# Strassen block products for twelve of 22 row tiles of a feed-forward down-projection, and for two more groups of the up-projection

## The chip, the cores and the metric

The kernel runs on one core of a Trainium2 chip. The metric is device microseconds of that core for one execution. TensorE multiplies matrices and writes to PSUM, which has eight banks of 128 x 512 fp32 here; VectorE (DVE), ScalarE (ACT) and GpSimd (POOL) work on tiles of 128 partitions; SyncE (SP) issues all DMAs.

## The reference

One layer of a model of width 1024 over 1024 tokens: RMS norm, a large input projection, sparse attention (8 heads) and an RWKV-7 recurrence side by side, their gated sum, an output projection with residual, and last a feed-forward part. Only the last is changed:

```python
def _conv_ffn(h, w_up, conv_w, w_down):
    u = h @ w_up                      # [1024, 1024] x [1024, 5632]
    u = causal depthwise convolution of u over tokens, width 3
    a, b = jnp.split(u, 2, axis=-1)   # 2816 columns each
    return (jax.nn.silu(a) * b) @ w_down   # [2816, 1024]

x = x + _conv_ffn(_rms_norm(x, norm_ffn), ffn_up, ffn_conv, ffn_down)
```

All is fp32.

## The kernel before, in words

**Precision.** Each fp32 operand is split in two fp32r tiles: hi is a ScalarE copy to fp32r, lo is the difference x - hi, on GpSimd for weights (lines 219, 1328) and on VectorE or GpSimd for data. A product is three matmuls of 128 x 128 by 128 x 512: hi hi, hi lo and lo hi (`mm3`, line 222). Tokens lie on the free axis in two halves of 512, h = 0 and 1.

**Order.** Instructions get a place on their engine from a planner, by priority (`tc.cur_priority`, program order within it) and the times it assumes; `tc.issue_after(x)` holds an instruction back behind x. Each engine then runs its list in order. A tile that takes the memory of another waits for that one's last reader.

**Up-projection.** The 2816 + 2816 columns are 22 groups: group i has output column tiles i and 22 + i (o = 0, 1), over k = 8 row tiles. The first `NE` = 12 groups are plain. Their half 0 is done by `ffn0(i)` (line 709), early: groups 0 to 7 (`NEW` = 8) as filler behind the recurrence, groups 8 to 11 at line 1250, at a lower priority than the norm of half 1 (lines 1238 to 1245), so that TensorE has work while VectorE, ScalarE and GpSimd normalize. Their half 1 is the loop at line 1341, one group after the other. Weights come as 512 KB tiles, three ahead, through `wslot` into a ring of four hi/lo slots, of which two lie in the pool `wp`, two in the pool `ffn` (opened at line 1255, when the norm's pools are closed). Raw weights alternate between two buffers in each pool (`wraw`). `taps` evacuates a bank with the convolution (one ScalarE and two VectorE operations of 512 columns, and two small ones for half 1), `silu` makes the gate and stores it to `th_d` in DRAM.

**Strassen groups.** Groups 12 to 21 are done for both halves at once by a Winograd form of Strassen's scheme: the weights as a 2 x 2 block matrix (output o by half of k), the data as one (half of k by token half), 7 block products in place of 8, 12 matmuls each (`prod`, loop at line 1394). Sums of weight blocks (`s12`, `s34`) are made by `prep_up`, sums of data blocks T1 to T4 once by `tprep` (per k tile 12 VectorE operations of 512 columns: 4 `summed`, 4 `diff`, 4 low parts), spread over the half-1 loop by `tsteps`.

**Down-projection** (line 1434). 22 row tiles in pairs. For each pair two gate tiles per half are loaded (`thr`), cut into hi (ScalarE, line 1445) and lo (GpSimd, line 1446), two weight tiles go through `wslot`, and 8 x 2 outputs of 6 matmuls each go through the banks of P and B (four); VectorE adds each bank to one of 16 running sums `acc` (line 1464), which begin as the residual `x2`. The last pair stores them.

Of the kernel before, what the change touches and what calls it, by code (L numbers as in the profile page):

```python
# [38 lines left out]
NZS = 3  # L39
# [92 lines left out]
def build(tc, D, dbg=None, upto=99):  # L132
# [7 lines left out]
    with ExitStack() as ctx:  # L140
# [1115 lines left out]

        def taps(u, o, i, h, pj, prev):
            ci = 22 * o + i
            A.activation(u, pj, AF.Copy, scale=P("conv", 88 + ci))  # L1259
            for d in (1, 2):  # L1260
                cw_ = P("conv", 44 * (2 - d) + ci)
                V.scalar_tensor_tensor(u[:, d:512], pj[:, 0:512 - d], cw_, u[:, d:512], op0=ALU.mult, op1=ALU.add)  # L1262
                if h:
                    V.scalar_tensor_tensor(u[:, 0:d], prev(d), cw_, u[:, 0:d], op0=ALU.mult, op1=ALU.add)  # L1264

        def silu(i, h, ua, ub):
            th = fp.tile([128, 512], F32, name="th", bufs=2)
# [72 lines left out]
        wq = [wslot(D["f_up"][22 * (n % 2) + n // 2]) for n in range(PFD)]  # L1340
        for i in range(NE):
            us = []
            for o in range(2):
                n = 2 * i + o + PFD
                if n < 2 * NE:
                    wq.append(wslot(D["f_up"][22 * (n % 2) + n // 2]))
                hi, lo = wq.pop(0)
                u = utile(o, 1)
                pj = ps("AM"[o])
                mm3(pj, hi, lo, h2hi[1], h2lo[1], 8)  # L1350
                taps(u, o, i, 1, pj, lambda d: cvl[:, i, o, 2 - d:2])
                us.append(u)
            t_ = silu(i, 1, *us)
            with tc.issue_after(t_):
                for k in tsteps[i]:
                    next(tg[k])

        def prod(bank, w, o_, xs_, start):
            n = 0
            for k, wi, xi in [(k, 0, x_) for k in range(4) for x_ in (0, 1)] + [(k, 1, 0) for k in range(4)]:  # L1360
                T.matmul(bank, w[wi][:, o_ + k], xs_[k][xi], start=start and n == 0, stop=n == 11,  # L1361
                         skip_group_check=True)
                n += 1

        b11 = [(h2hi[0][k], h2lo[0][k]) for k in range(4)]
        b21 = [(h2hi[0][k], h2lo[0][k]) for k in range(4, 8)]
        b22 = [(h2hi[1][k], h2lo[1][k]) for k in range(4, 8)]
        lo4, hi4 = slice(0, 4), slice(4, 8)

        def prep_up(i):  # L1370
# [13 lines left out]
            w["b"] = split8(rb, wp, wp, "whi", "wlo", hi4, bufs=2)  # L1384
            yield

        def tmp(name, tag, n):
            return FP["f"].tile([128, 512], F32, name=name, tag=tag, bufs=n)

        g_ = prep_up(NE)  # L1390
        w = next(g_)
        for _ in range(3):
            next(g_)
        for i in range(NE, 22):
            g_ = prep_up(i + 1) if i < 21 else iter([None] * 4)
            pa, pb, pc, pd_ = ps("P"), ps("M"), ps("A"), ps("B")
            prod(pa, w["a"], 0, b11, True)
            p1 = tmp("p1", "zs", NZS)
            A.activation(p1, pa, AF.Copy)
            prod(pb, w["12"], 4, TB[2], True)  # L1400
            u2 = tmp("u2", "fu", 3)
            V.tensor_add(u2, pb, p1)  # L1402
            prod(pa, w["a"], 4, b21, False)
            wn = next(g_)
# [12 lines left out]
            prod(pb, w["b"], 4, TB[4], False)  # L1417
            next(g_)
            V.tensor_add(pb, pb, p1)
            taps(u[1][0], 1, i, 0, pb, None)  # L1420
# [5 lines left out]
        acc = {}  # L1426
        for m in range(8):
            for h in range(2):
                if m < 4:
                    acc[m, h] = hp2.tile([128, 512], F32, name=f"acc{m}{h}", tag=f"{('h2hi', 'h2lo')[h]}_{m}")  # L1430
                else:
                    acc[m, h] = fp.tile([128, 512], F32, name=f"acc{m}{h}", tag=f"T3{'hl'[h]}{m - 4}")
        GR = 2
        for g0 in range(0, 22, GR):
            hd_, wd_ = [], []
            for i in range(g0, g0 + GR):
                raw = fp.tile([128, 2, 512], F32, name="thr", tag=("s12", "s34")[i % 2])
                j = i % 4
                hs = []
                for h in range(2):  # L1440
                    load(raw[:, h], th_d[h][i])
                    tn = (2, 1)[j // 2], 2 * (j % 2) + h
                    hi = fp.tile([128, 512], FR, name="hh", tag="T%dh%d" % tn)
                    lo = fp.tile([128, 512], FR, name="hl", tag="T%dl%d" % tn)
                    A.activation(hi, raw[:, h], AF.Copy)  # L1445
                    G.tensor_sub(lo, raw[:, h], hi.bitcast(F32))  # L1446
                    hs.append((hi, lo))
                hd_.append(hs)
                wd_.append(wslot(D["f_dn"][i]))
            if g0 == 0:  # L1450
                with tc.issue_after(lastw[0]):
                    for m in range(8):
                        for h in range(2):
                            load(acc[m, h], x2_d[h][m])
            for m in range(8):
                for h in range(2):
                    pj = ps("PB"[h])
                    n = 0
                    for hs, (dh, dl) in zip(hd_, wd_):
                        hh, hl = hs[h]  # L1460
                        for a, b in ((dh, hh), (dh, hl), (dl, hh)):
                            T.matmul(pj, a[:, m], b, start=(n == 0), stop=(n == 3 * GR - 1))  # L1462
                            n += 1
                    V.tensor_add(acc[m, h], acc[m, h], pj)  # L1464
                    if g0 + GR >= 22:
                        nc.sync.dma_start(D["out"][m][:, H[h]], acc[m, h])
        fst.close()
        hst[1].close()

# [16 lines left out]
```

## Time and profile before

| | before |
|---|---|
| runs, median (lowest to highest) | 1855.0 us (1852.8 to 1855.7), 3 runs |
| the profiled execution | 1852.6 us, of which 1850.8 us is the span of the profile |
| mean granted TensorE clock | 0.989 of 2.4 GHz |
| TensorE busy | 1786.8 us, 97% of the span |
| VectorE, ScalarE, GpSimd busy | 1100.7, 824.4, 706.2 us |

The span goes from the first to the last instruction. Busy time of matmuls counts pipelined instructions, so a busy TensorE still needs the count beside it: matmuls started per microsecond. A wait is shown with what ended it. In the rows, L225 is line 225 of the kernel; names such as `psP` are tiles (`psP`: a PSUM bank with tag P), the form follows as output from input.

### The profile page before, as it was taken

The numbers are of one execution on the slowest core, as the hardware profiler recorded it, in microseconds if no ns is written. First come the engines' busy times: TensorE is split into PE (matmuls) and PEld (weight loads), VectorE is DVE, ScalarE is ACT, GpSimd is POOL, SyncE is SP. The second block draws the span as 40 slices with busy tenths as digits, with TensorE's granted clock in tenths as the row PEclk, the third lists the DMA queues.
The fourth block names the chain that finished last, engine by engine and source line by source line (L and its number), as shares of the span: only waits on it lengthen the run. The fifth ranks groups of instructions, "written<-read, shape, count | busy, mean of one in ns | idle before, by whom it ended". The sixth has DMA issues, their size and how long they took to land. (4 is left out here: it accounts for less than half of the span.)

```text
span 1850.8 us, 30936 instructions
## 1 busy us (share of the span) xinstructions
PE 1786.8 (97%) x11986; PEld 1389.8 (75%) x11986; DVE 1100.7 (59%) x1933; ACT 824.4 (45%) x1512; POOL 706.2 (38%) x454
## 2 busy tenths in 40 slices
PE   8999999999999999999999899999999999999999
PEld 5885657777777787777777678878877888888887
DVE  6214666768766503974444354347998988844444
ACT  5234765657555632545555454343344444411220
POOL 5222032141233335212145455555443444644441
PEclk9999999999999999999999899999999999999999
DMA  5415053232333346255453465334332223622222
GB/s 177 125 52 186 29 170 96 81 114 60 125 132 126 126 136 229 97 172 169 158 171 120 144 226 167 123 108 143 114 114 91 80 80 102 240 91 92 91 69 91
DMA packets 134019, 232.29 MB, mean 126 GB/s; under 512 B 25072, under 2 KB 54128, under 8 KB 133616
## 3 DMA queue, kind: packets, MB, share of 16 engines
q1 hardware_dynamic: 133872, 230.31, 38.0%
q8 instruction: 94, 1.54, 0.3%
q14 instruction: 53, 0.43, 0.1%
HBM read 161.48 MB, written 63.96 MB: 122 GB/s over the span
## 5 line engine op out<-in xcount | busy, mean ns | idle before, releaser
L219 POOL TENSOR_TENSOR wlo<-wraw,whi 128x1024 fp32r<-128x1024 f32 (+1 forms) x110 | 241.2, 2197 | 419.8 <-ACT whi L218 147.5
L225 PE MATMUL psP<-hhi,whi 128*128 128x512 f32 x816 | 333.6, 410 | 14.0 <-ACT hhi L705 8.1
L225 PE MATMUL psP<-hlo,whi 128*128 128x512 f32 x816 | 330.1, 405 | 3.8 <-DVE hlo L706 2.5
L225 PE MATMUL psP<-hhi,wlo 128*128 128x512 f32 x816 | 215.2, 397 | 0.0
L225 PEld LDWEIGHTS psP<-hhi,whi 128*128 128x128 f32 x816 | 156.2, 192 | 52.6 <-ACT hhi L705 9.9
L225 PEld LDWEIGHTS psP<-hlo,whi 128*128 128x128 f32 x816 | 156.5, 192 | 40.3 <-DVE hlo L706 3.8
L225 PEld LDWEIGHTS psP<-hhi,wlo 128*128 128x128 f32 x816 | 151.1, 188 | 32.7 <-issue 0.5
L218 ACT ACTIVATE whi<-wraw 128x1024 fp32r<-128x1024 f32 (+1 forms) x110 | 106.0, 964 | 130.0 <-PE psP L225 79.9
L542 DVE TENSOR_TENSOR pl<-pf,ph 128x512 f16<-128x512 f32 (+3 forms) x208 | 123.6, 603 | 43.8 <-ACT pf L541 42.9
L540 ACT ACTIVATE ph<-psA 128x512 f16<-128x512 f32 (+3 forms) x208 | 99.2, 477 | 61.7 <-PE psA L535 43.4
L483 DVE TENSOR_REDUCE mp<-psM 128x1 f32<-128x512 f32 (+1 forms) x192 | 94.4, 514 | 42.7 <-PE psM L481 35.9
L1328 POOL TENSOR_TENSOR wlo<-wraw,whi 128x1024 fp32r<-128x1024 f32 (+1 forms) x43 | 99.0, 2302 | 44.9 <-ACT whi L1327 32.6
L1446 POOL TENSOR_TENSOR hl<-thr,hh 128x512 fp32r<-128x512 f32 x44 | 57.9, 1329 | 114.8 <-ACT hh L1445 114.8
L1445 ACT ACTIVATE hh<-thr 128x512 fp32r<-128x512 f32 x44 | 27.2, 625 | 163.9 <-PE psB L1462 160.3
L541 ACT ACTIVATE pf<-psA 128x512 f32<-128x512 f32 (+3 forms) x208 | 99.7, 479 | 0.0
L1464 DVE TENSOR_TENSOR acc<-acc,psP 128x512 f32<-128x512 f32 x88 | 60.5, 687 | 59.3 <-PE psP L1462 59.3
L1464 DVE TENSOR_TENSOR acc<-acc,psB 128x512 f32<-128x512 f32 x88 | 60.5, 687 | 59.3 <-PE psB L1462 59.3
L545 PEld LDWEIGHTS <-ph 128*128 128x128 f16 x592 | 55.8, 97 | 22.5 <-issue 12.5
L550 PEld LDWEIGHTS <-pl 128*128 128x128 f16 x592 | 55.4, 98 | 20.5 <-DVE pl L542 6.3
L564 POOL TENSOR_TENSOR onat<-onat,ot 128x256 f32<-128x256 f32 x32 | 25.0, 783 | 111.8 <-DVE ot L563 88.8
L720 DVE SCALAR_TENSOR_TENSOR fu<-psP,par,fu 128x511 f32<-128x511 f32 (+1 forms) x48 | 35.8, 747 | 41.1 <-ACT cvl L718 40.4
L1269 ACT ACTIVATE th<-u 128x512 f32<-128x512 f32 x32 | 20.1, 627 | 84.8 <-issue 70.5
(472 smaller groups left out, 4594.4 us busy)
## 6 DMA issues: line engine op xcount, KB each, us to landing
wraw<-f_up SPq DMA_DIRECT2D x68, 512.0 KB, 3.4
wraw<-w_t SPq DMA_DIRECT2D x46, 512.0 KB, 3.9
wraw<-f_dn SPq DMA_DIRECT2D x22, 512.0 KB, 4.1
thr<-th_d SPq DMA_DIRECT2D x44, 256.0 KB, 4.1
sg_d<-zs SPq DMA_DIRECT2D x32, 256.0 KB, 2.0
wraw<-w_out SPq DMA_DIRECT2D x16, 512.0 KB, 3.4
th_d<-th SPq DMA_DIRECT2D x32, 256.0 KB, 2.1
z_d<-zs SPq DMA_DIRECT2D x28, 256.0 KB, 2.4
```

Of the source, the lines that this page charges most:

```text
L218: A.activation(hi[:, :nk], raw, AF.Copy)
L219: G.tensor_sub(lo[:, :nk], raw, hi[:, :nk].bitcast(F32))
L225: T.matmul(ps, a[:, k], ks_(b, k), start=(n == 0), stop=(n == 3 * nk - 1))
L483: V.reduce_max(mp[:, x, br, t:t + 1], pm[:, 0:(b1 - b0) * 128], axis=AX.X)
L540: A.activation(ph[0:nkey, rg], pa[0:nkey, rg], AF.Exp, scale=0.125)
L541: A.activation(pf[0:nkey, rg], pa[0:nkey, rg], AF.Exp, scale=0.125)
L542: V.tensor_sub(pl[0:nkey, rg], pf[0:nkey, rg], ph[0:nkey, rg])
L545: T.matmul(pov[:, t, :], ph[0:nkey, tk], vt[0:nkey, kb, g, 0:65], start=first, stop=False, skip_group_check=True)
L550: T.matmul(pov[:, t, :], pl[0:nkey, tk], vt[0:nkey, kb, g, 0:65], start=False, stop=True, skip_group_check=True)
L1328: G.tensor_sub(lo[:, ks], raw[:, ks], hi[:, ks].bitcast(F32))
L1446: G.tensor_sub(lo, raw[:, h], hi.bitcast(F32))
L1464: V.tensor_add(acc[m, h], acc[m, h], pj)
```

## The change

`NE` goes from 12 to 10: groups 10 and 11 of the up-projection become Strassen groups; `ffn0` and the half-1 loop have two groups less. The twelve entries of `tsteps` become ten. In the half-1 loop the gate of group i - 1 comes behind the taps of group i, and the first Strassen group's weights are prepared in the loop's last round.

The down-projection goes through `DSEQ` = "nnsnsnsn": n is a plain pair of row tiles (`plain`), s is a set of four (`combined`), so 5 x 2 plain and 3 x 4 combined. In a set the weights are a 2 x 2 block matrix (row tiles by output half), the gates another (row tiles by token half). There are 7 products of 4 outputs with 6 matmuls each: `product(o1)` ("a"), o2, o5 ("e"), o6 ("b"), o7 ("d"), o3, o4. o2, o3 and o4 are added to `acc` at once; the four others have running sums `sacc` over the three sets (the first set copies them by ScalarE), which `merge` adds into `acc` in the last set. `operands` cuts weights (ScalarE, GpSimd) and data (ScalarE, and GpSimd or VectorE); block sums are made on VectorE, queued in `todo` and let go one by one behind the bank sums (`tick`). All eight banks are used in turn, for plain pairs too. Rings: four weight slots, twelve places for data.

```diff
-NE, NEW = 12, 8
+NE, NEW = 10, 8
+DSEQ = "nnsnsnsn"
...
-        tsteps = [(), (0,), (0,), (0, 1), (1,), (), (1, 2), (2,), (2, 3), (3,), (3,), ()]
+        tsteps = [(), (0,), (0,), (0, 1), (1,), (1, 2), (2,), (2, 3), (3,), (3,)]
...
         for i in range(NE):
             us = []
+            if i == NE - 1:
+                g_ = prep_up(NE)
+                w = next(g_)
+                next(g_)
             for o in range(2):
...
-            t_ = silu(i, 1, *us)
-            with tc.issue_after(t_):
+            if i:
+                silu(i - 1, 1, *prev)
+            prev = us
+            with tc.issue_after(lasts[0]):
                 for k in tsteps[i]:
                     next(tg[k])
+        silu(NE - 1, 1, *prev)
...
+        def tick(ins):
+            if todo:
+                with tc.issue_after(ins.ins):
+                    todo.pop(0)()
...
+        def cut(dst, src, e):
+            A.activation(dst[0], src, AF.Copy)
+            e.tensor_sub(dst[1], src, dst[0].bitcast(F32))
...
+        def combined(i0, first, last):
...
+            def sums(n_):
+                for kp in range(2):
+                    def tsum(kp=kp):
+                        b11, b12, b21, b22 = B[kp]
+                        t = tt[kp][n_] = f32t(FP["f"], FT, [128, 512], "tq")
+                        x, y = ((b12, b11), (b22, tt[kp][0]), (b22, b12), (b21, tt[kp][1]))[n_]
+                        V.tensor_sub(t, x, y)
...
+                    todo.extend([tsum, wsum])
+
+            def operands(wsrc, bsrc, eb):
+                w = slot()
+                for kp in range(2):
+                    cut([x[:, 4 * kp:4 * kp + 4] for x in w], wsrc[kp], G)
+                hs = pset(2)
+                for kp in range(2):
+                    cut(hs[kp], bsrc[kp], eb)
+                return w, hs
+
+            def product(ops_, n_, key, first=False):
+                w, hs = ops_
+                for j in range(4):
+                    pj = ps("PBAM"[j])
+                    n = 0
+                    for kp in range(2):
+                        for x, y in ((0, 0), (0, 1), (1, 0)):
+                            T.matmul(pj, w[x][:, 4 * kp + j], hs[kp][y], start=(n == 0), stop=(n == 5))
+                            n += 1
+                    if key is None:
+                        d = sacc[n_, j]
+                        if first:
+                            A.activation(d, pj, AF.Copy)
+                            continue
+                    else:
+                        d = acc[key[0] + j, key[1]]
+                    tick(V.tensor_add(d, d, pj))
...
+            yield
+            with tc.issue_after(t_):
+                o1 = operands([W[k][0][:, lo4] for k in range(2)], [B[k][0] for k in range(2)], G)
+                o2 = operands([W[k][1][:, lo4] for k in range(2)], [B[k][2] for k in range(2)], G)
+            sums(0)
+            sums(1)
+            yield
+            flush()
+            sums(2)
+            sums(3)
+            product(o1, "a", None, first)
+            o5 = sop(0, G)
+            product(o2, None, (0, 0))
+            flush()
+            if last:
+                merge(0)
+            o6 = sop(1, V)
+            product(o5, "e", None, first)
+            o7 = sop(2, V)
+            product(o6, "b", None, first)
+            if last:
+                merge(1)
+            o3 = operands([ss[k][3] for k in range(2)], [B[k][3] for k in range(2)], G)
+            product(o7, "d", None, first)
+            if last:
+                merge(2)
+            o4 = operands([W[k][1][:, hi4] for k in range(2)], [tt[k][3] for k in range(2)], V)
+            yield
+            product(o3, None, (0, 1))
+            product(o4, None, (4, 0))
...
+        for n in range(len(seq)):
+            if DSEQ[n] == "n" and n + 1 < len(seq):
+                next(seq[n + 1])
+                if DSEQ[n + 1] == "s":
+                    next(seq[n + 1])
+                next(seq[n], None)
+            elif DSEQ[n] == "n":
+                next(seq[n], None)
+                flush()
+            else:
+                next(seq[n])
+                if n + 1 < len(seq):
+                    next(seq[n + 1])
+                next(seq[n], None)
```

## Rows read from the trace of the kernel before

**Rows 1.** The profile page: span, and busy time of each engine (share of span).

```profile
span 1850.8 us, 30936 instructions
...
PE 1786.8 (97%) x11986; PEld 1389.8 (75%) x11986; DVE 1100.7 (59%) x1933; ACT 824.4 (45%) x1512; POOL 706.2 (38%) x454
```

**Rows 2.** Windows: each engine's busy time (instructions) per stretch; granted clock, DMA last.

```profile
1100.00:1150.00 50.00, 50.00 (x220) 41.13 (x220) 22.23 (x30) 20.62 (x35) 27.57 (x14) 1.00 0.47 147
1265.00:1405.00 140.00, 138.22 (x603) 112.43 (x602) 125.33 (x164) 52.88 (x78) 65.81 (x26) 1.00 0.36 120
1405.00:1596.00 191.00, 187.77 (x816) 152.36 (x815) 168.59 (x244) 81.32 (x114) 91.37 (x44) 1.00 0.29 100
1604.00:1847.00 243.00, 243.00 (x1048) 196.41 (x1046) 124.66 (x186) 39.59 (x57) 93.94 (x57) 1.00 0.28 94
```

**Rows 3.** TensorE's timeline, 1234 to 1250 us: start, length, instruction, idle before.

```profile
1240.28 0.77 PE L225 MATMUL psP<-hhi,whi 128*128 128x512 f32 x1 [3.90 <-DVE fu L720]
...
1248.60 0.47 PE L225 MATMUL psP<-hhi,whi 128*128 128x512 f32 x1
```

**Rows 4.** TensorE's waits from 1265 to 1420 us: total, times, longest.

```profile
PE psP L1361 <- ACT p L1399: 1.3, 1, 1.3
PE psM L1361 <- DVE u L1402: 1.1, 1, 1.1
PE psM L225 <- DVE u L1264: 0.9, 1, 0.9
```

**Rows 5.** Groups by line, 1605 to 1840 us: busy us, mean ns | idle before.

```profile
L1464 DVE TENSOR_TENSOR acc<-acc,psP 128x512 f32<-128x512 f32 x85 | 58.4, 687 | 57.2 <-PE psP L1462 57.2
...
L1446 POOL TENSOR_TENSOR hl<-thr,hh 128x512 fp32r<-128x512 f32 x36 | 46.4, 1299 | 113.2 <-ACT hh L1445 113.2
...
L1445 ACT ACTIVATE hh<-thr 128x512 fp32r<-128x512 f32 x36 | 22.5, 624 | 160.9 <-PE psB L1462 160.3
...
L1328 POOL TENSOR_TENSOR s12l<-wraw,s12h 128x1024 fp32r<-128x1024 f32 x5 | 12.0, 2402 | 0.0
```

**Rows 6.** VectorE's timeline, 1839 to 1851 us, the last sums.

```profile
1847.23 0.69 DVE L1464 TENSOR_TENSOR acc<-acc,psP 128x512 f32<-128x512 f32 x1 [0.70 <-PE psP L1462]
```

**Rows 7.** SyncE's DMA issues from 1245 to 1261 us.

```profile
1254.66 0.33 SPq L727 DMA_DIRECT2D th_d<-zs  x1
1255.09 2.17 SPq L138 DMA_DIRECT2D wraw<-f_up  x3
```

**Rows 8.** ScalarE's timeline over the same stretch.

```profile
1260.37 1.06 ACT L1327 ACTIVATE s12h<-wraw 128x1024 fp32r<-128x1024 f32 x1 [2.97 <-DMA wraw<-f_up]
```

**Rows 9.** VectorE's timeline from 1246 to 1256 us.

```profile
1248.98 2.89 DVE L1243 SCALAR_TENSOR_TENSOR hf<-x,par,rstd 128x512 f32<-128x512 f32 x1
...
1253.95 0.69 DVE L726 SCALAR_TENSOR_TENSOR zs<-zs,fu 128x512 f32<-128x512 f32 x1
```

**Rows 10.** Line 1292, whole run: duration ns min/median/max, first and last start.

```profile
L1292 DVE TENSOR_TENSOR T3l<-t,T3h x4: 682/684/685, 1306.8 to 1395.1; 128x512 fp32r<-128x512 f32 x4
```

**Rows 11.** GpSimd's timeline from 1246 to 1256 us.

```profile
1248.87 2.45 POOL L219 TENSOR_TENSOR wlo<-wraw,whi 128x1024 fp32r<-128x1024 f32 x1 [3.54 <-ACT whi L218]
1252.61 1.30 POOL L1245 TENSOR_TENSOR h2lo<-hf,h2hi 128x512 fp32r<-128x512 f32 x1 [1.29 <-ACT h2hi L1244]
```

**Rows 12.** The profile page: DMA issues, count, KB each, median us to landing.

```profile
wraw<-f_up SPq DMA_DIRECT2D x68, 512.0 KB, 3.4
```

**Rows 13.** Windows: TensorE alone while it starts again; granted clock after the brackets.

```profile
1240.00:1246.00 6.00, 5.72 (x14) 0.50 0.00 0
```

**Rows 14.** Groups by line, 1275 to 1390 us, the half-1 loop.

```profile
L1297 DVE TENSOR_TENSOR t<-zs 128x512 f32<-128x512 f32 x8 | 14.1, 1791 | 0.0
...
L1297 DVE TENSOR_TENSOR t<-zs,t 128x512 f32<-128x512 f32 x8 | 11.7, 1468 | 0.1
...
L1285 DVE TENSOR_TENSOR zs<-h2hi,h2lo 128x512 f32<-128x512 f32 x6 | 8.5, 1422 | 0.0
...
L1285 DVE TENSOR_TENSOR zs<-hhi,hlo 128x512 f32<-128x512 f32 x8 | 6.4, 797 | 2.2 <-DMA th_d<-zs 2.2
```

More of the change, by code (lines that the diff above doesn't have):

```diff
@@ L1264, in taps @@
                     V.scalar_tensor_tensor(u[:, 0:d], prev(d), cw_, u[:, 0:d], op0=ALU.mult, op1=ALU.add)
+            return a_.ins
         def silu(i, h, ua, ub):
@@ L1424, in build @@
             w = wn
-        acc = {}
-        for m in range(8):
+        for m in range(4, 8):
             for h in range(2):
[L1429 to L1434, printed above, removed]
+                acc[m, h] = fp.tile([128, 512], F32, name=f"acc{m}{h}", tag=f"T3{'hl'[h]}{m - 4}")
@@ new lines, in build, with flush, pset @@
+        pring = [0]
+        todo = []
+        def tick(ins):
+            if todo:
+                with tc.issue_after(ins.ins):
+                    todo.pop(0)()
+        def flush(keep=0):
+            while len(todo) > keep:
+                todo.pop(0)()
+        def pset(n):
+            r = []
+            for _ in range(n):
+                p = pring[0] % 12
+                pring[0] += 1
+                r.append([fp.tile([128, 512], FR, name="hh" + c, tag="T%d%s%d" % ((2, 1, 4)[p // 4], c, p % 4))
+                          for c in "hl"])
+            return r
@@ L1435, in build, with slot, plain @@
+        def slot():
+            n = wn_[0] % 4
+            wn_[0] += 1
+            if n % 2 == 0:
+                return [wp.tile([128, 8, 128], FR, name=t, bufs=2) for t in ("whi", "wlo")]
+            return [fp.tile([128, 8, 128], FR, name=t) for t in (("s12h", "s12l"), ("s34h", "s34l"))[n // 2]]
+        def cut(dst, src, e):
+            A.activation(dst[0], src, AF.Copy)
+            e.tensor_sub(dst[1], src, dst[0].bitcast(F32))
+        def plain(i0):
             hd_, wd_ = [], []
-            for i in range(g0, g0 + GR):
+            for i in (i0, i0 + 1):
@@ L1448, in build @@
-                hd_.append(hs)
[L1449 to L1454, printed above, removed]
+                    with tc.issue_after(t_) if i0 == 2 else ExitStack():
+                        cut(hs[h], raw[:, h], G)
+                hd_.append(hs)
+                w = slot()
+                cut(w, wraw(D["f_dn"][i]), G)
@@ new lines, in merge, with m0, m1, m2 @@
+        def merge(part):
+            for j in range(4):
+                a_, b_, d_, e_ = (sacc[n_, j] for n_ in "abde")
+                def m0(j=j, a_=a_):
+                    V.tensor_add(acc[j, 0], acc[j, 0], a_)
+                def m1(a_=a_, b_=b_):
+                    V.tensor_add(b_, a_, b_)
+                def m2(j=j, b_=b_, d_=d_):
+                    G.tensor_add(d_, b_, d_)
+                    G.tensor_add(acc[4 + j, 0], acc[4 + j, 0], d_)
+                def m3(b_=b_, e_=e_):
+                    V.tensor_add(b_, b_, e_)
+                def m4(j=j, b_=b_, d_=d_, e_=e_):
+                    V.tensor_add(acc[j, 1], acc[j, 1], b_)
+                    G.tensor_add(d_, d_, e_)
+                    G.tensor_add(acc[4 + j, 1], acc[4 + j, 1], d_)
+                todo.extend(((m0,), (m1,), (m2, m3, m4))[part])
@@ new lines, in build @@
+        seq, i0 = [], 0
+        for c in DSEQ:
+            if c == "n":
+                seq.append(plain(i0))
+                i0 += 2
+            else:
+                seq.append(combined(i0, "s" not in DSEQ[:len(seq)], "s" not in DSEQ[len(seq) + 1:]))
+                i0 += 4
+        assert i0 == 22
+        lastc = len(DSEQ) - 1 - DSEQ[::-1].index("s")
+        next(seq[0])
+        for m in range(4, 8):
+            for h in range(2):
+                load(acc[m, h], x2_d[h][m])
+        for n in range(len(seq)):
[7 more added lines that the diff above has]
+                flush()
+            else:
+                next(seq[n])
+                if n + 1 < len(seq):
+                    next(seq[n + 1])
+                next(seq[n], None)
```

120 lines of the change are left out of this document (78 added, 42 removed).

## Prediction

> **What bounds the kernel.** I read the page first: TensorE is busy in 97% of the span [rows 1], so a change can pay only by taking matmuls away or idle time, and costs only where it makes TensorE wait. Next the windows: in a stretch with nothing else, 220 matmuls fill 50 us, 0.227 us each; in the down-projection 1048 fill 243 us, 0.232 us each; the granted clock is 1.00 (2.4 GHz) in both [rows 2]. Then TensorE's timeline and waits over the feed-forward part, from 1219 us on. It idles there at three places: 3.9 us at 1236 while half 1 is normalized [rows 3], six short waits at the end of the half-1 loop and at the first Strassen group (4.4 us together, the longest shown [rows 4]), and nowhere in the down-projection, where VectorE's sums follow each bank by 0.7 us and wait for TensorE [rows 5, 6]. The reader should see that VectorE is not far behind: 125.3 of 140 us in the half-1 loop and 168.6 of 191 in the Strassen groups, but half of the down-projection [rows 2].
>
> **Matmuls removed.** A plain up-projection group is 2 halves x 2 outputs x 24 = 96 matmuls, a Strassen group 7 products x 12 = 84. Two groups change: 24 x 0.227 = 5.5 us. In the down-projection four row tiles are 4 x 48 = 192 plain, and 7 products x 4 x 6 = 168 combined; three such sets save 72 x 0.232 = 16.7 us. Together 22.2 us. The Trainium skill (TensorE: Matmul & The Clock Gate, Back-to-back issue gap) gives about 131 ns for each matmul of 512 columns in a stream with weight loads; by that an estimate for 96 would be 12.6 us. The windows here give 227 to 232, and the measurement decides.
>
> **The cover that goes with NE = 10.** Of each group, 48 matmuls (half 0) are the `ffn0` filler; groups 8 to 11 run behind the last w_out matmul while half 1 is normalized. The last one of group 9 ends at 1248.6, when group 10 begins [rows 3]; groups 10 and 11, 96 matmuls, go. What is next then are half 1's own groups, and their weights are not there: the two loads into the `ffn` pool are issued at 1255.09, behind the store of group 9's gate at 1254.66 [rows 7], and the first conversion of such a tile starts at 1260.37 [rows 8]. That pool is opened where the pools of the norm are closed, so I take the loads to wait for the norm's last readers. After the change part of this moves up: the last norm product took 2.89 us where an unhindered step takes about 0.7 [rows 9, 10], because it ended with GpSimd's split of group 10's weights [rows 11], which is gone. So group 9's gate and store come 2.2 us earlier, at 1252.5, the load at 1252.9; a load lands in 3.4 us [rows 12], the conversion is 1.06: 1257.4, or 8.8 us after 1248.6. If the load goes ahead of the store, as the norm allows at about 1250, it is 6 us. I take 8. Then the clock: behind the 3.9 us idle the granted clock was 0.50 (1.2 GHz) for 6 us, with 14 matmuls in it [rows 13] where 26 would fit, so 12 x 0.227 = 2.8 us. Taken: +11. Bounds: +1 if the weights are already there (only the last norm tile is waited for), +16 if the loads stay where they were, so that the conversion that ends at 1261.4 is the first (12.8 idle, and 2.8).
>
> **The half-1 loop.** It goes from 12 groups (131 us of TensorE) to 10 (109), with all 48 VectorE steps that make T1 to T4 still in it. Those are 16 of line 1297 and 16 of line 1285, 40.7 us for the 30 that the window holds, 1.36 each [rows 14], and 16 of line 1292 at 0.68 [rows 10]: 54 us. The rest of VectorE's 125.3 [rows 2] is 71 over 12 groups, 5.9 each. After: 59 + 54 = 113 against 109. VectorE becomes the longer one by 4 us, and it was already what TensorE waited for here [rows 4]. Gating one group later puts the taps, which free the banks, ahead of the gate and fills the wait for the tanh; preparing group 10 inside the loop covers some of the 2.4 us at its end. I take +4: bounds -4.4 (all six waits go) and +10 (about one group's lead of two banks is lost once).
>
> **The combined sets.** VectorE: 28 sums at 0.69 [rows 5], 16 weight and data differences and 6 low parts at 0.68 [rows 10]: 34.3 us of 168 x 0.232 = 39.0. GpSimd: 14 weight cuts and 8 data cuts of 512 columns at 1.30: 28.6; ScalarE: 28 x 0.62 = 17.5 [rows 5]. A plain pair behind it is 22.3 us of TensorE with 11.0 of VectorE and 4 x 1.30 + 2 x 2.40 = 10.0 of GpSimd. Each fits alone: over set and pair 45.3 and 38.6 of 61.3. What the rows do not show is how the two get on, for the 22 VectorE steps that read two SBUF tiles are the kind that stood behind GpSimd in the norm [rows 9, 11] and in lines 1297 and 1285, while sums from PSUM kept 0.687 beside 94 us of GpSimd [rows 2, 5]. In the half-1 loop 32 such steps averaged 0.68 over the free time, with GpSimd busy 47% by pieces of 2.4 us [rows 2, 5]; with 63% by pieces of 1.3 that is about 0.5. 22 x 0.5 = 11: VectorE 56 of 61. The eight banks now used hold 8 x 1.39 = 11 us of lead, and the first two operands and eight differences are made in the pair ahead. So the steady sets are hidden. The last one also merges: 16 sums on VectorE (10.9) and 16 on GpSimd (20.8), into its last products and the last pair: 67 of 61 for VectorE, minus the lead. Taken: +2; below 0, above +27 (third rival). Loads are the same bytes; the end (one sum and a store [rows 6]) is unchanged.
>
> **Sum.** 1852.6 (profiled execution, span 1850.8) - 22.2 + 11 + 4 + 2 = 1847.4. The median of the runs, 1855.0, lies 2.4 above that execution; I split the difference and say 1848.5.
>
> **Rivals.**
> First, all the waits are hidden: the weights of half 1 are loaded during the norm, and the later gates free VectorE. For it: nothing in the rows names memory as what held the loads. Against: the queue was otherwise idle and they still came at 1255. -22.2 + 1 to 5 - 4 to 0: 1827 to 1840.
>
> Second, the up-projection eats the gain: +13 at the norm and +8 in the loop, while the down-projection does as forecast: 1852.6 - 22.2 + 13 + 8 + 2 = 1853, no change; with both bounds met in full it is 1858. For it: VectorE is at 90% of that loop now [rows 2]. Against: both have to come near their worst.
>
> Third, VectorE and GpSimd take turns in the sets. Each of 22 steps then waits a whole cut: 22 x 1.98 + 19.3 = 62.9 against 39.0; with the pair 73.9 against 61.3, three times 12.6, less the first set's 16 copies that ScalarE makes (11.0): +27, so 1872. It decides for "slower" when the mean wait passes 0.9 us (0.73 is what set and pair hide; 66 waits share the other 11). For it: single steps of 2.9 us in the norm [rows 9]. Against: GpSimd has 38.6 of 61 to do, so it can't be there at each step. The Trainium skill (GPSIMD Engine Reference, Specifications) says that GpSimd contends with VectorE's instructions of two SBUF inputs; the trace agrees, with 1.79 us for a step of 0.68 [rows 10, 14].
>
> **Chances.** Forecast (1841 to 1851): 0.39. First rival: 0.21. Second: 0.17. Third, or a smaller form of it above 1859: 0.23. Runs of this kernel differ by 0.15%, so 0.2% (3.7 us) is what can be told from no change. Faster 0.60, same 0.17, slower 0.23. Leaving out the fastest tenth and the far end of the third gives 1835 to 1865; for the forecast alone it is 1841 to 1851.
>
> **What would show it.** TensorE idle of 6 to 10 us about 1249, then a stretch at clock 0.50; the half-1 loop at 109 to 115 us with waits on `u`; 840 + 168 = 1008 matmuls in Strassen groups, 984 in the down-projection at about 0.23 us; waits there under 3 us, with lines of `tensor_sub` on VectorE near 1.2 us. No idle at 1249 would make the first rival right; waits of TensorE on VectorE in every set, with those lines near 2 us, the third. A down-projection that saves less than 10 us breaks the forecast.

## The result, and the profile after

The median went from 1855.36 to 1831.41 us (1828.12 to 1837.01, six runs); the ratio is 0.988, with a 95% interval of 0.9856 to 0.9904. The profiled execution took 1830.07 us. I had said 1848.5, between 1835 and 1865: the sign was right, the gain is nearly four times the forecast one, and it is the case of the first rival that came true.

The page of the kernel after, its span and the busy time of each engine:

```profile
span 1828.3 us, 30848 instructions
...
PE 1764.1 (96%) x11890; PEld 1375.4 (75%) x11890; DVE 1168.6 (64%) x2005; ACT 856.7 (47%) x1574; POOL 773.4 (42%) x500
```

It shows 96 matmuls less and all the other engines busier [rows 1]. The windows of after (half-1 loop, Strassen groups, down-projection without its end, and two pieces of the end):

```profile
1252.00:1364.00 112.00, 111.54 (x482) 91.49 (x483) 106.59 (x137) 47.90 (x65) 63.15 (x23) 0.98 0.36 127
1364.00:1596.00 232.00, 231.87 (x1015) 190.07 (x1014) 208.91 (x304) 96.97 (x139) 112.06 (x52) 1.00 0.30 104
...
1604.00:1780.00 176.00, 176.00 (x774) 145.05 (x773) 135.50 (x179) 64.66 (x111) 115.11 (x79) 1.00 0.28 96
...
1780.00:1800.00 20.00, 19.39 (x81) 14.37 (x79) 20.00 (x25) 3.28 (x5) 18.75 (x12) 1.00 0.08 27
1800.00:1807.00 7.00, 5.04 (x16) 4.02 (x17) 7.00 (x8) 0.00 (x0) 7.00 (x5) 0.76 0.00 0
```

Against [rows 2] the reader should see three things. VectorE is busy in 106.6 of 112 us of the loop and in 208.9 of 232 of the Strassen groups, and yet TensorE has no gap there that the view of waits shows. In the down-projection 774 matmuls fill 176 us, 0.227 each, where it was 0.232. And after 1780 VectorE and GpSimd are full, and TensorE is not. TensorE's waits after 1225 us (total, times, longest) are only these:

```profile
PE psM L226 <- ACT s34h L1329: 4.0, 1, 4.0
PE psP L226 <- DVE fu L721: 3.9, 1, 3.9
PE psP L1499 <- POOL wlo L1476: 2.3, 1, 2.3
```

The second was there before [rows 3]; the six of the loop and the first Strassen groups [rows 4] are gone; the first and the third are new.

**An account.** Up to the statistics of the feed-forward norm (the last matmul `psP<-sq,ones`, line 697 after) both programs do the same, and this untouched part took 1044 to 1059 us in the profiled executions. So I compare from that matmul on, in three stretches of TensorE's timeline: A to the first product with T2, B to the last matmul of the up-projection, C to the last matmul of all. They come from one profiled execution of each kernel. B was 229.6 us in all eight kernels that share its order and its buffers. A repeats less well: it was 316.1 to 318.0 us in the six kernels that differ only behind it (after, e2, e7 to e10), so a difference of 2 us in A says nothing by itself. Each ratio is against runs of the kernel before that were taken beside that kernel (their medians were 1855.4, 1856.2, 1855.2 and 1852.6 us); for kernels of different groups the ratios compare better than the medians.

| kernel | median us | ratio, 95% interval | A | B | C | sum |
|---|---|---|---|---|---|---|
| before | 1855.4 | | 360.3 | 196.0 | 242.9 | 799.2 |
| after | 1831.4 | 0.988 (0.9856 to 0.9904) | 317.8 | 229.6 | 228.0 | 775.4 |
| e1_banks | 1854.8 | 0.9996 (0.9982 to 1.0011) | 360.0 | 196.1 | 242.7 | 798.8 |
| e2_up_only | 1847.8 | 0.9949 (0.9932 to 0.9967) | 317.9 | 228.7 | 245.1 | 791.7 |
| e3_down_only | 1840.0 | 0.991 (0.989 to 0.9929) | 361.2 | 196.1 | 226.8 | 784.1 |
| e4_new6 | 1829.0 | 0.9845 (0.9822 to 0.9868) | 315.3 | 229.6 | 226.9 | 771.8 |
| e5_raw_first | 1830.5 | 0.986 (0.9835 to 0.9885) | 317.8 | 233.1 | 226.5 | 777.4 |
| e6_gates_now | 1838.6 | 0.9911 (0.988 to 0.9942) | 319.9 | 234.1 | 228.4 | 782.4 |
| e7_two_plain_last | 1834.4 | 0.9878 (0.9854 to 0.9902) | 316.1 | 229.6 | 233.0 | 778.7 |
| e8_cuts_on_vector | 1831.2 | 0.987 (0.9839 to 0.99) | 316.6 | 229.6 | 227.8 | 774.0 |
| e9_no_merge | 1825.4 | 0.9854 (0.983 to 0.9878) | 317.8 | 229.6 | 222.5 | 769.9 |
| e10_late_merge | 1829.7 | 0.9878 (0.9855 to 0.9901) | 318.0 | 229.6 | 225.3 | 772.9 |
| e11_late_new6 | 1824.9 | 0.985 (0.9828 to 0.9873) | 315.6 | 229.6 | 225.2 | 770.4 |
| e12_new6_cuts | 1829.2 | 0.9859 (0.9834 to 0.9883) | 315.6 | 229.6 | 226.8 | 772.0 |

In each stretch I split the distance from one matmul's start to the next into the usual one (0.228, or 0.232) and what goes beyond it where it is over 0.30 (idle time and slow clock together). From before to after: -22.3 for the matmuls; +4.4 at the norm, where the excess rose from 7.6 to 12.0 us between 1215 and 1268; -5.4 from there to 1420, where it fell from 6.3 to 0.9; +5.4 at the end, from 0; and about -5 because matmuls follow each other faster, 4.0 of it in C (976 x 4.1 ns). That is -22.9 of the measured -23.8. The norm's and the end's parts hold for these two executions; in others of the table they differ by 1 to 2 us.

### The profile page after: what moved, and what is told of

The parts are those of the page before. It is cut to its first block, busy times and chain, and to the rows that moved or that the text cites. A ratio compares the mean times of both kernels' runs of the same rounds, so it can differ in the third digit from the quotient of the medians.

```text
span 1828.3 us, 30848 instructions
## 1 busy us (share of the span) xinstructions
PE 1764.1 (96%) x11890; PEld 1375.4 (75%) x11890; DVE 1168.6 (64%) x2005; ACT 856.7 (47%) x1574; POOL 773.4 (42%) x500
## 4 chain that ended last, share of the span: by engine, by line
PE 40%; DVE 7%; issue 1%; ACT 1%; DMA 1%; POOL 1%; POOLq 0%; DVEq 0%; SPq 0%; ACTq 0%
PE psP L226 9%; PE psM L1389 5%; PE psA L1389 3%; PE psP L1389 3%; PE psA L226 3%; PE psB L1499 2%; PE psA L1499 1%; PE psM L1499 1%; PE psP L1499 1%; PE psB L226 1%; PE psP L1570 1%; DVE u L1265 1%; PE psA L1570 1%; PE psM L1570 1%; PE psB L1570 1%
## 5 line engine op out<-in xcount | busy, mean ns | idle before, releaser
L220 POOL TENSOR_TENSOR wlo<-wraw,whi 128x1024 fp32r<-128x1024 f32 (+1 forms) x106 | 231.1, 2185 | 409.1 <-ACT whi L219 151.2
L226 PE MATMUL psP<-hhi,whi 128*128 128x512 f32 x784 | 319.3, 408 | 15.1 <-ACT hhi L706 8.9
L226 PE MATMUL psP<-hlo,whi 128*128 128x512 f32 x784 | 316.1, 404 | 3.8 <-DVE hlo L707 2.4
L226 PE MATMUL psP<-hhi,wlo 128*128 128x512 f32 x784 | 208.5, 399 | 0.0
L226 PEld LDWEIGHTS psP<-hhi,whi 128*128 128x128 f32 x784 | 149.3, 191 | 51.3 <-ACT hhi L706 10.6
L226 PEld LDWEIGHTS psP<-hlo,whi 128*128 128x128 f32 x784 | 149.3, 191 | 38.9 <-DVE hlo L707 3.8
L219 ACT ACTIVATE whi<-wraw 128x1024 fp32r<-128x1024 f32 (+1 forms) x106 | 101.8, 961 | 131.6 <-PE psP L226 76.8
L1330 POOL TENSOR_TENSOR wlo<-wraw,whi 128x1024 fp32r<-128x1024 f32 (+1 forms) x34 | 73.5, 2163 | 54.8 <-PE psM L1389 20.3
L546 PEld LDWEIGHTS <-ph 128*128 128x128 f16 x592 | 55.8, 97 | 22.6 <-issue 12.3
L1329 ACT ACTIVATE whi<-wraw 128x1024 fp32r<-128x1024 f32 (+1 forms) x34 | 30.8, 910 | 64.1 <-issue 29.7
L549 PEld LDWEIGHTS <-ph 128*128 128x128 f16 x592 | 56.1, 98 | 2.1 <-issue 2.0
L1273 DVE SCALAR_TENSOR_TENSOR th<-th,u 128x512 f32<-128x512 f32 x34 | 56.8, 1670 | 0.4
L1330 POOL TENSOR_TENSOR s34l<-s,s34h 128x1024 fp32r<-128x1024 f32 x12 | 30.0, 2498 | 61.5 <-ACT s34h L1329 61.5
```

What stands on the lines that cost most here:

```text
L219: A.activation(hi[:, :nk], raw, AF.Copy)
L220: G.tensor_sub(lo[:, :nk], raw, hi[:, :nk].bitcast(F32))
L226: T.matmul(ps, a[:, k], ks_(b, k), start=(n == 0), stop=(n == 3 * nk - 1))
L1273: V.scalar_tensor_tensor(th, th, 0.5, ub, op0=ALU.mult, op1=ALU.mult)
L1330: G.tensor_sub(lo[:, ks], raw[:, ks], hi[:, ks].bitcast(F32))
```

## The experiments

**e1_banks: eight banks on the old down-projection.** The old plain pairs take the banks in the order of the new ones, nothing else; it asks whether the faster spacing comes from the banks.

```diff
-                    pj = ps("PB"[h])
+                    pj = ps("PBAM"[(2 * m + h) % 4])
```

> The kernel before, with its plain down-projection going through all eight PSUM banks (P, B, A, M in turn) in place of four. Theory A (bank turn): matmuls of the down-projection followed each other at 232 ns before and at 228 ns in the changed kernel, in its plain pairs too, because each bank rests for eight groups of six matmuls rather than four; then the spacing here falls to about 228 ns and 1056 x 4 ns = 4 us are gained, some 1851. Rival B (something else in the new down-projection, the places of the data tiles or the planner's order): the spacing stays at 232 ns and the time at 1855.

Ratio 0.9996, and the spacing stayed at 232.2 ns. The number of banks alone does not bring the closer spacing.

**e2_up_only: the up-projection's part alone**, with its later gates and early preparation, on the old down-projection (the diff is against the kernel before; the later ones are against after).

```diff
-NE, NEW = 12, 8
+NE, NEW = 10, 8
...
-            t_ = silu(i, 1, *us)
-            with tc.issue_after(t_):
+            if i:
+                silu(i - 1, 1, *prev)
+            prev = us
+            with tc.issue_after(lasts[0]):
```

> The up-projection's part of the change alone (NE = 10, ten steps, gates one group later, first Strassen weights prepared in the loop), on the old down-projection. Theory A (from the trace of the changed kernel): 24 matmuls less is -5.5 us, the uncovered norm costs about +4.5, and the six waits at the end of the loop, with their slower start, go for -5: about -6, some 1849. Rival B (the forecast): -5.5 + 11 + 4 = +9.5, some 1865.

It gained 7.5 us from the statistics to the end (1856.2 to 1847.8 in medians), where my steps gave a loss. The matmuls are 5.5 of it; fewer waits and a closer spacing are the rest. Its waits, in the same view as above:

```profile
PE psM L225 <- ACT s34h L1328: 4.0, 1, 4.0
PE psP L225 <- DVE fu L720: 3.9, 1, 3.9
PE psP L1468 <- DVE acc L1470: 0.6, 1, 0.6
```

**e3_down_only: the down-projection's part alone**, with the up-projection of before (the diff is against the kernel after).

```diff
-NE, NEW = 10, 8
+NE, NEW = 12, 8
...
-            if i:
-                silu(i - 1, 1, *prev)
-            prev = us
-            with tc.issue_after(lasts[0]):
+            t_ = silu(i, 1, *us)
+            with tc.issue_after(t_):
...
-        silu(NE - 1, 1, *prev)
```

> The down-projection's part alone, with the twelve plain up-projection groups, gates and steps of before. Theory A: 72 matmuls less (-16.5), closer spacing (-4), and 6 us lost at the end, where the last set's merges make VectorE and GpSimd late: -14.5, some 1840, with the loss at the end in the same place. Rival B (the forecast): -16.7 + 2 = -14.7, with the waits spread over the sets; the time does not tell the two apart, the spacing and the place of the waits do. Together with the up-projection's part alone it also shows whether the two parts add up to the whole (-22 to -24).

It gained 15.1 us, and its waits are those of both kernels: the loop's are back, the one at the end is there. The four longest of nine:

```profile
PE psP L226 <- DVE fu L721: 3.9, 1, 3.9
PE psP L1494 <- POOL wlo L1471: 2.3, 1, 2.3
PE psP L1363 <- ACT p L1410: 1.4, 1, 1.4
PE psM L1363 <- DVE u L1413: 1.1, 1, 1.1
```

The two parts add up: -7.5 - 15.1 = -22.6 against -23.8 together. The missing waits of the loop belong to the up-projection's part, the loss at the end to the down-projection's.

**e4_new6: four groups behind the norm.** With NEW = 6, groups 6 to 9 are the filler, as many as before the change.

```diff
-NE, NEW = 10, 8
+NE, NEW = 10, 6
```

> The changed kernel with NEW = 6, so that again four filler groups run behind the norm of half 1; everything else and the number of matmuls are the same. Theory A (the uncovered norm costs some 4.5 us at 1249 us): TensorE's idle there goes and the changed kernel gains about 4 us, some 1827. Rival B: the two groups that move were covering something earlier, behind the recurrence, and idle time opens there instead; no gain, some 1831.

The wait for `s34h` is gone, and the excess at the norm is 7.6 us again, as before: 4.4 less than after. A new wait of 1.0 us at 1168 takes part of it back, so A is 2.5 us shorter, and the whole from the statistics to the end 3.6, of which 1.1 lie in C, behind the edit. A was 315.3 to 315.6 us in the three kernels with NEW = 6 (e4, e11, e12), below all six with NEW = 8 and the same loop. The cover that NE = 10 took away was worth about 4.4 at the norm in these executions, not 11.

**e5_raw_first: another raw tile first.** The counter that chooses the raw buffers starts two later, so that the first two weight tiles of half 1, not the third and fourth, come through `wp`.

```diff
-        rn_ = [1]
+        rn_ = [3]
```

> The changed kernel with the ring of raw weight buffers begun one step further (rn_ from 1 to 3), so that the first two weight tiles of half 1 land in the pool that is always there, and the third and fourth in the pool that opens behind the norm. Theory A (TensorE's idle of 4 us at 1249 us ends when the first tile of that later pool can be written, behind the norm's last low part): the first group's weights are then ready before the norm is done, the idle falls under 1.5 us, and about 4 us are gained from the norm to the end. Rival B (the norm itself or the clock sets the restart): the idle stays near 4 us, no gain.

TensorE's idle time behind the filler fell from 4.0 to 1.6 us, near what the theory wanted (under 1.5); that rest is the norm's last low part. Nothing was won, which the theory had not foreseen. The waits over 0.3 us between 1215 and 1400 us:

```profile
PE psP L226 <- DVE fu L721: 3.9, 1, 3.9
PE psP L1389 <- ACT p L1415: 1.9, 1, 1.9
PE psA L226 <- POOL h2lo L1246: 1.6, 1, 1.6
PE psM L226 <- DVE u L1263: 0.6, 1, 0.6
PE psA L226 <- DVE u L1265: 0.5, 1, 0.5
```

My reading is that the idle time had been VectorE's lead: TensorE was about 1.5 us earlier in the loop, waited there and at the first Strassen group, and B became 3.5 us longer. No run isolates this, for the edit also moves every later raw tile of the up-projection to another buffer.

**e6_gates_now: the gates behind their own taps** again, with the T sums let go behind the gate, all else as after.

```diff
-            if i:
-                silu(i - 1, 1, *prev)
-            prev = us
-            with tc.issue_after(lasts[0]):
+            t_ = silu(i, 1, *us)
+            with tc.issue_after(t_):
...
-        silu(NE - 1, 1, *prev)
```

> The changed kernel with each gate of the half-1 loop right behind its own taps, as before; the loop still has ten groups and the first Strassen weights are still prepared in it. Theory A (the later gate and the early preparation are what keeps VectorE off TensorE's path, though VectorE is busy over 95% of the loop): TensorE waits for VectorE again in the loop and at the first Strassen group, 3 to 8 us in all, which is my forecast of +4 for the loop. Rival B (the six waits went because of the early preparation alone, or because VectorE's work began during the idle at 1249): no wait over 1 us, same time.

7.0 us more than after from the statistics to the end; the ratios, 0.9911 and 0.988, say the same, though their intervals overlap a little. But only 4.5 of the 7.0 us stand where the edit acts: TensorE waits 3.48 us at the first product with T2 and then runs seven matmuls at the slow clock. Another 1.2 stand just behind the statistics and 1.2 at the norm, with no change of order there. ScalarE's timeline shows what the wait was for:

```profile
1384.76 0.63 ACT L1271 ACTIVATE th<-u 128x512 f32<-128x512 f32 x1 [5.84 <-issue]
1385.30 0.61 ACT L1293 ACTIVATE T2h<-t 128x512 fp32r<-128x512 f32 x1
```

The conversion of the last tile of T2 stands in ScalarE's list behind the tanh of the last group's gate. VectorE had made its input by 1371.5, but the tanh waited until 1384.7 for the taps, which a full VectorE finished then. In the kernel after, where the gate comes one group later, the tanh finds its input done, and the conversion follows at once:

```profile
1365.34 0.62 ACT L1271 ACTIVATE th<-u 128x512 f32<-128x512 f32 x1
1365.86 0.62 ACT L1293 ACTIVATE T2h<-t 128x512 fp32r<-128x512 f32 x1
```

The edit moves the gate and the release of the T sums together; which of the two matters more is open.

**e7_two_plain_last: the last set earlier,** with its merges still inside it and two plain pairs behind.

```diff
-DSEQ = "nnsnsnsn"
+DSEQ = "nsnsnsnn"
```

> The changed kernel with DSEQ nsnsnsnn: the same three sets and five pairs, but two plain pairs behind the last set. Theory A (the 6 us lost from 1780 us on come from the last set's merges, which crowd VectorE and GpSimd wherever the set stands): the slow stretch and the wait for a low part of weights move some 22 us earlier and stay, no gain; only the first set, with less plain work ahead, may lose 1 to 3 us. Rival B (they come from the end, where the last pair's cuts and the merges meet and no slack is left): the loss falls below 2 us and about 4 us are gained.

C became 5.0 us longer (3.3 from the statistics on, since A was 1.7 shorter; the instructions of A stand in the same order as after, so the edit gives no reason for that). The wait for `wlo` moved with the set, to 1781.74, and grew to 3.44 us; the first set, now with one pair ahead of it, had waits of 0.76 and 0.73 on VectorE's sums.

**e8_cuts_on_vector: all low parts of a set's data on VectorE.**

```diff
-                o1 = operands([W[k][0][:, lo4] for k in range(2)], [B[k][0] for k in range(2)], G)
+                o1 = operands([W[k][0][:, lo4] for k in range(2)], [B[k][0] for k in range(2)], V)
...
-            o5 = sop(0, G)
+            o5 = sop(0, V)
```

The same is done for o2 and o3.

> The changed kernel with all low parts of data in the sets on VectorE: eight steps per set go from GpSimd (10.4 us) to VectorE (5.4 us). Theory A (VectorE and GpSimd only hinder each other step by step, 0.4 us a step, and the eight banks cover it): VectorE's busy time rises to near 60 of 61 us for a set and a pair, TensorE begins to wait in the sets, 2 to 8 us slower in all. Rival B (GpSimd is the one that is late, as in the wait for a low part of weights near the end): fewer cuts on GpSimd, the wait near the end goes, same or 2 to 4 us faster.

C was 227.8 against 228.0: no difference, which neither theory had said. VectorE had the room, and the wait for `wlo` was still 2.3 us: GpSimd's cuts of the data are not what makes it late.

**e9_no_merge: the last set without its merges.** It leaves the running sums out of the output.

```diff
             if last:
-                merge(0)
+                pass
...
-                merge(1)
+                pass
...
-                merge(2)
+                pass
```

> The changed kernel without the merges: the running sums a, b, d and e of the sets are made but never added into the outputs, so 16 sums on VectorE and 16 on GpSimd are left out. Theory A (the merges in the last set are what costs TensorE the 5.9 us after 1780): no wait for a low part of the last weight tile, no spacings of 400 to 530 ns after 1780, the stretch from the last plain pair but one to the end 5 to 6 us shorter, median 1825 to 1827. Theory B (the last set is slow by its own cuts, block sums and bank sums): the wait of 2.3 us stays and the time changes by under 1.5 us, 1830 to 1832.

C fell by 5.5 us, with no excess left in it. GpSimd's last cut begins at once when its input is there:

```profile
1786.03 2.42 POOL L1476 TENSOR_TENSOR wlo<-wraw,whi 128x1024 fp32r<-128x1024 f32 x1 [0.51 <-ACT whi L1475]
```

So the loss at the end comes with the merges, all of it.

**e10_late_merge: the merges behind the last set,** let go one by one in two plain pairs.

```diff
-DSEQ = "nnsnsnsn"
+DSEQ = "nsnsnsnn"
...
             product(o4, None, (4, 0))
+            if last:
+                merge(0)
+                merge(1)
+                merge(2)
```

The three calls of `merge` between the products go.

> The changed kernel with two plain pairs last and all merges queued behind the last set, one let go behind each bank sum of these two pairs; no work is left out. Over the two pairs VectorE has 32 bank sums of 0.67 and 24 merge steps of about 1.2, 50 of 44.6 us if every step is let go at once, less whatever is still left at the end; GpSimd 16 merge steps of 1.74 and the cuts of one pair, 28 + 10 = 38 of 44.6. Theory A (what costs is that merges stand beside the set's cuts and sums): most of the 5.9 us comes back, 1826 to 1829, and the earlier order of two plain pairs last with merges inside the set (3.3 us slower than the changed kernel) is beaten by 6 to 8 us. Theory B (VectorE's and GpSimd's total behind the last product decides): the merges now end later than TensorE, and the last stores wait for them; 1833 to 1840.

C was 225.3: 7.7 less than with the merges inside the set (e7) and 2.7 less than after. An excess of 2.5 is left in it, all at 1618 to 1625, in the first set, which here has one plain pair ahead of it in place of two; the merges themselves cost nothing now:

```profile
PE psM L1570 <- DVE acc L1501: 0.8, 1, 0.8
PE psA L1570 <- DVE acc L1501: 0.8, 1, 0.8
```

From the statistics to the end e10 is 5.8 us shorter than e7. The ratios of their runs don't show it (both 0.9878 of before, with intervals of 0.0023 or 4 us to either side), so it rests on one profiled execution of each.

**e11_late_new6 and e12_new6_cuts: repairs together.** e11 is e10 with NEW = 6, e12 is e8 with NEW = 6.

```diff
-NE, NEW = 10, 8
+NE, NEW = 10, 6
```

> The same with four groups of the up-projection left behind the norm in place of two. If both repairs hold and add (idle at the norm gone: -3.6 measured before; merges late: -5), 1822 to 1826. If the late merges fail, -3.6 against the kernel with late merges alone; if what the norm gives is lost later, as with the raw tile put first, the same as the kernel with late merges alone.

> The changed kernel with four groups left behind the norm and all low parts of a set's data on VectorE. Theory A (each is independent: -3.6 at the norm, -1.4 in the down-projection): 1826 to 1828, the wait of 2.3 us for the last weight's low part still there. Theory B (the second was only the norm's idle in another place): the same as with four groups alone, 1828 to 1830.

e11: 5.0 us less than after from the statistics to the end, and the lowest sum of the kernels that do all the work; by ratios to before it (0.985) can't be told from e4 (0.9845), and its interval overlaps that of after. e12: 0.2 more than e4, so the 1.4 us that e8 had seemed to win lay in A, at the norm, and theory B holds.

## Why the prediction was wrong

Two steps failed, the half-1 loop (+4 forecast, -5.4 measured) and the cover at the norm (+11, +4.4); one term was missing (the spacing, -5 in all), and the sets cost 3.4 more than I took.

**Matmuls removed: right.** 22.2 forecast, -22.3 in the account.

**The cover at the norm: this step failed, in size.** I took +11, it was +4.4: 4.0 us of idle time for the 8 that I took, and 0.4 for the clock's 2.8. The step says of half 1's weights: "their weights are not there". For two of the first four tiles the raw data was there. TensorE's timeline after the filler:

```profile
1252.45 0.80 PE L226 MATMUL psM<-h2hi,s34h 128*128 128x512 f32 x1 [3.97 <-ACT s34h L1329]
1253.05 0.63 PE L226 MATMUL psM<-h2lo,s34h 128*128 128x512 f32 x1
```

What comes first is a product with `s34h`, the fourth weight slot. SyncE's issues and ScalarE's conversions tell why:

```profile
1228.01 8.53 SPq L139 DMA_DIRECT2D wraw<-f_up  x2
...
1251.34 3.87 SPq L139 DMA_DIRECT2D wraw<-f_up  x3
1255.43 0.33 SPq L728 DMA_DIRECT2D th_d<-zs  x1
```

```profile
1251.34 1.06 ACT L1329 ACTIVATE s34h<-wraw 128x1024 fp32r<-128x1024 f32 x1 [2.08 <-POOL h2lo L1246]
...
1254.87 2.02 ACT L1329 ACTIVATE whi<-wraw 128x1024 fp32r<-128x1024 f32 x2 [2.47 <-DMA wraw<-f_up]
```

Raw buffers and hi/lo slots alternate on their own. The slot `s34h` lies in the pool `ffn`, but the raw tile that feeds it lies in `wp`, and its load went out at 1236.20, during the norm, as the second of the first row's two. (The first of them is, by the order of the buffers, the third tile's; its conversion stood behind the first tile's in ScalarE's list.) Only the conversion to `s34h` waited, for the norm's last low part on GpSimd (1247.87, 3.44 us). I had counted `ffn` as one thing, and had not asked which of the four tiles is free of it and whether the planner can put its product first. The other loads came as I had allowed for, ahead of the gate's store, at 1251.34 rather than 1255.09 [rows 7], and the first conversions behind them began at 1254.87, where I had the load at 1252.9; nobody was idle for it. e4 agrees with the size. The +1 of the first rival, nothing but the norm's last tile, was too good: in e5 that tile alone left 1.6 us of idle time.

The clock did not add its 2.8. TensorE in 6 us behind each of the two idle times of after:

```profile
1241.00:1247.00 6.00, 5.86 (x19) 0.72 0.12 44
1252.40:1258.40 6.00, 5.95 (x20) 0.73 0.84 291
```

Of the 26 matmuls that fit, 7 and 6 are missing, 13 together; before, 12 were missing behind the one idle time [rows 13]. In e10, whose order at the norm is the same, only 13 matmuls ran from 1254 to 1260, at 0.50, and the excess at the norm was 13.4 for the 12.0 of after. So the clock's small share was in part luck.

**The half-1 loop: this step failed, wrong in sign.** +4 forecast, -5.4 measured. I set VectorE's total (113) against TensorE's (109) and let the longer one decide. VectorE came out at 106.6 of 112 us, for two reasons. Its T sums began at 1248.3, while TensorE idled at the norm, and they were cheaper, 49.0 us for the 54 that I had worked out (all T sums but the 16 low parts at 0.68, after):

```profile
L1299 DVE TENSOR_TENSOR t<-zs,t 128x512 f32<-128x512 f32 x8 | 11.9, 1489 | 0.1
L1287 DVE TENSOR_TENSOR zs<-h2hi,h2lo 128x512 f32<-128x512 f32 x8 | 9.7, 1237 | 0.0
L1287 DVE TENSOR_TENSOR zs<-hhi,hlo 128x512 f32<-128x512 f32 x8 | 8.8, 1094 | 4.1 <-DMA th_d<-zs 4.0
L1299 DVE TENSOR_TENSOR t<-zs 128x512 f32<-128x512 f32 x8 | 7.7, 992 | 0.0
```

But the main point is order, not VectorE's total: e6 has the same work on VectorE as after and loses 4.5 us by its order alone, to one wait behind ScalarE's list. I had named the later gates and counted them for little. That the six waits of before went for the same reason is argued, not shown: e6's wait is another one, and no run has the early preparation of group 10 alone. e5 may be the other side: where TensorE comes 1.5 us earlier, it meets VectorE, so the loop would be near its balance.

**The sets: the price of contention was right, the place of the loss right, its size short.** VectorE's steps of two SBUF tiles inside the sets:

```profile
L1476 DVE TENSOR_TENSOR hhl<-tq,hhh 128x512 fp32r<-128x512 f32 x18 | 19.6, 1088 | 5.2 <-ACT hhh L1475 5.2
L1538 DVE TENSOR_TENSOR tq<-thq 128x512 f32<-128x512 f32 x12 | 16.4, 1370 | 0.0
L1538 DVE TENSOR_TENSOR tq<-thq,tq 128x512 f32<-128x512 f32 x12 | 12.7, 1055 | 0.0
```

The 66 such steps, those that sum weights too, average 1.05 us, a wait of 0.4 where I had estimated 0.5; the third rival needed 0.9 to decide and 1.3 for its +27. There is no wait in the steady sets. The merges cost 5.4, not 2: I had balanced VectorE over set and pair together, but most of the loss came from GpSimd's list, in which the last pair's weight cut stood behind five merge steps (1.3 to 1.84 us each; my own 38.6 and 20.8 make 59.4 of 61.3 us for GpSimd, a sum that the step never formed):

```profile
1790.67 1.30 POOL L1626 TENSOR_TENSOR sd<-sb,sd 128x512 f32<-128x512 f32 x1 [0.63 <-DVE sb L1623]
1792.60 1.30 POOL L1626 TENSOR_TENSOR sd<-sb,sd 128x512 f32<-128x512 f32 x1 [0.63 <-DVE sb L1623]
1793.86 1.74 POOL L1627 TENSOR_TENSOR acc<-acc,sd 128x512 f32<-128x512 f32 x1
1795.57 1.74 POOL L1626 TENSOR_TENSOR sd<-sb,sd 128x512 f32<-128x512 f32 x1
1797.27 1.84 POOL L1627 TENSOR_TENSOR acc<-acc,sd 128x512 f32<-128x512 f32 x1
1799.06 2.85 POOL L1476 TENSOR_TENSOR wlo<-wraw,whi 128x1024 fp32r<-128x1024 f32 x1
```

TensorE needed that tile at 1799.6, got it at 1801.96, and then ran seven matmuls at the slow clock (0.76 granted over 1800 to 1807). The rest of the 5.4 are distances of 0.41 to 0.53 us at 1781 to 1787, where it waited for banks that VectorE was late to empty (1782.08, for one, came 0.06 us behind VectorE's sum from that tag).

**What no step had.** The spacing in the down-projection, -4.0. I took 0.232 from [rows 2] for both sides.

With the measured terms in place of mine, 1852.6 - 22.3 + 4.4 - 5.4 + 5.4 - 5 = 1829.7, and the profiled execution took 1830.07. That it comes so near is partly luck: 0.9 us of the stretches have no term, and the untouched part was 1.1 us longer in that execution. The first rival's range held the result, in part because the +5.4 and the -5 that it didn't have cancel. It had the mechanism of the loop right as far as e6 goes (the later gates) and that of the norm in part; it lost its weight to one sentence, that the loads "still came at 1255", which was true of tiles that nobody had to wait for. The 0.15% that I gave for the scatter of the runs was also too small: the kernel before ran from 1847.4 to 1862.3 us in later groups of runs.

## What to carry to other kernels

When a filler goes, look at every tile that the next product could start from, with the buffer that its raw data passes through; one that is ready is enough if the order may change. A loop in which an engine is nine tenths busy and TensorE still waits is first a question of which instruction stands ahead of which in each list: here moving a gate, and the T sums behind it, was worth 4.5 us (e6), nearly as much as the 5.5 us of matmuls removed beside it. Work that has no one waiting for it (merges) should not be queued ahead of work that has, on any engine; put behind the last set (e10), the merges cost nothing that the traces show.

## What the runs showed of the hardware that was not expected

The same instructions run at two spacings, both with a granted clock of 1.00. Matmuls of plain pairs followed each other every 232.2 ns in before, e1 and e2, and every 227.8 to 228.9 in after. In the last pair, of the same code in the same order, it was 227.8 to 228.2 ns in after, e5 and e7 to e11, and 231.8 to 232.0 in e3, e4, e6 and e12; in e3 it changed from pair to pair (232.3, 227.8, 227.8, 231.8). The pattern differs too: six matmuls of one bank in the last pair took 227, 226, 226, 230, 231 and 227 ns in after, and 236, 228, 233, 236, 229 and 232 in e12. It isn't the number of banks alone (e1); the cause stays open, and with it 4 us of the difference.

VectorE's step of two SBUF tiles took 0.68 us alone [rows 10], 1.05 on the mean of 66 in the sets and 1.41 twice beside GpSimd's pieces of 1.3 us (1791.11 and 1793.04 of after), while its sums from a bank kept 0.67 in the same microseconds (1784 to 1800). The Trainium skill (GPSIMD Engine Reference, Specifications) names VectorE's instructions with two SBUF inputs among those that contend with GpSimd; the trace agrees.

Which of the two engines waits can differ between programs that are alike up to there. At the end of the norm the same instructions in the same order stand side by side in after (first two lines) and e7 (last two):

```profile
1247.87 3.44 POOL L1246 TENSOR_TENSOR h2lo<-hf,h2hi 128x512 fp32r<-128x512 f32 x1 [3.21 <-ACT h2hi L1245]
1248.30 1.28 DVE L1287 TENSOR_TENSOR zs<-h2hi,h2lo 128x512 f32<-128x512 f32 x2
1245.54 1.67 POOL L1246 TENSOR_TENSOR h2lo<-hf,h2hi 128x512 fp32r<-128x512 f32 x1 [3.21 <-ACT h2hi L1245]
1245.98 2.38 DVE L1287 TENSOR_TENSOR zs<-h2hi,h2lo 128x512 f32<-128x512 f32 x2
```

In e7 GpSimd's step is 1.8 us shorter and VectorE's two are 1.1 us longer; TensorE then waited 1.8 us for `s34h`, not 4.0, and 1.7 us for VectorE later. e8 is like e7 (1.64 and 2.35), and e2, e6, e9 and e10 are like after. So nearly 2 us of the idle time at the norm in after hang on which of the two was held up; what decides it the traces do not show.
